# Shifts and scales of the second sub-layer computed with features on partitions

## Chip, cores and metric

The program runs on one core of one Trainium2 chip. The metric is device time in microseconds (us) of one launch, the median of several runs.

## What is computed

One decoder layer on 512 tokens of width 1024. A conditioning vector c gives, for each of the two sub-layers (token mixing and MLP), a shift, a scale and a gate of 1024 numbers each: six rows of a 1024 by 6144 product. Cut to what matters:

```python
c_act = jax.nn.silu(c)
mod = c_act @ w_ada[l] + b_ada[l]
sh1, sc1, g1, sh2, sc2, g2 = jnp.split(mod, 6, axis=-1)
h = rmsnorm(x, norm_gains[l, 0]) * (1.0 + sc1) + sh1
y = token_mixer(h, ...)                    # 8 block-sparse heads, 8 sliding-window heads
x = x + g1 * rmsnorm(y, norm_gains[l, 1])
h = rmsnorm(x, norm_gains[l, 2]) * (1.0 + sc2) + sh2
y = square(relu(h @ w1 + b1)) @ w2 + b2
x = x + g2 * rmsnorm(y, norm_gains[l, 3])
```

The change concerns sh2 and sc2 alone, 2048 dot products of length 1024. The code calls the two sub-layers "layer" 0 and 1.

## The kernel before

Every large product is made of three fp32r matmuls (high by high, high by low, low by high parts, lines 96 to 98), so that each weight tile is split on the way: ACT copies the high part (line 83), POOL or DVE subtracts to get the low part (line 85).

The stages in order of time: the first modulation and the first projections (to about 57 us), then a loop over 64 blocks of attention (lines 802 to 867; 16 heads of 4 blocks of 128 queries; about 63 to 207 us), then the output projection, the residual and the second norm (to about 262 us), then the two MLP products (to about 586 us) and the output.

In the attention loop PE follows the order of the program. In step k it issues the transposes of the block three or four steps back (line 649), the scores of block k (lines 618 and 619), now and then a head's output (line 676), and then matmuls of a "filler" worth 1450 ns (900 ns from k = 24 on): the remaining projections, and later the output projection. The other engines' orders are fixed at build time by a planner that simulates the schedule. A block's chain is: PE scores; DVE adds the bias and takes the minimum (line 626); ACT takes exponentials (line 633); DVE reciprocal (line 639); POOL normalises (line 640); PE transposes. For sliding-window heads POOL first copies a column into the tile (line 617).

Beside this chain run the "side" steps, one call of next(side) each (lines 763 to 776). `ada_wide` computes 1024 sums over the 1024 features of c with c's features on partitions: for each of 8 chunks of c, two DVE instructions of 128x512 (lines 260 and 262) multiply a raw tile by one column of silu(c) and add to `adaacc`; each is one call. What is then left is a sum over the 128 partitions. For a gate (`gate_row`) PE does it with a matmul by ones (line 277). For the second sub-layer's shifts and scales (two units of 1024, r = 1 and 2) PE transposes the eight 128x128 pieces of the accumulator (line 225) and DVE reduces them from PSUM (line 226); `ada_cols` then adds the bias, and forms (1 + scale) * gain with four one-column instructions (line 237). The raw tiles rotate through four buffers (tag araw), and the accumulator has one (tag adaacc).

Calls 1 to 16 are the gate; call 17 closes it and does the first half of unit 1; calls 17 to 32 are unit 1, 33 to 48 unit 2 (33 closes unit 1), 49 closes unit 2. How many calls are made by step k is set in `side_at` (line 773). Each call's DVE instructions are placed in DVE's queue behind the bias instruction of the same step (`behind`).

The first sub-layer's shifts and scales are already computed the other way, in `ada_dot` (line 305): features on partitions, one DVE multiply-and-sum of 128x1024 against silu(c) held on every partition (c_bc).

Of the kernel before, what the change touches and what calls it, by code (L numbers as in the profile page):

```python
# [21 lines left out]
F32 = mybir.dt.float32  # L22
F32R = mybir.dt.float32r
AF = mybir.ActivationFunctionType
ALU = mybir.AluOpType

P = 128
DM = 1024
S = 512
NT = S // P  # L30
KC = DM // P
# [12 lines left out]


@with_exitstack
def layer_kernel(ctx, tc, x, c_col, ada_c, ada_r, bada_col, bada_row, gain_col, gain_row, w_in0, w_in1, w_in2,
                 w_out, w1, b1_col, w2, b2_row, rel, sinks, onehot, out):
    nc = tc.nc

    const = ctx.enter_context(tc.tile_pool(name="const", bufs=1))
    dram = ctx.enter_context(tc.tile_pool(name="dram", bufs=1, space=bass.MemoryType.DRAM))
    small = ctx.enter_context(tc.tile_pool(name="small", bufs=4))
    keep = ctx.enter_context(tc.tile_pool(name="keep", bufs=1))
    wts = ctx.enter_context(tc.tile_pool(name="wts", bufs=2))
# [4 lines left out]
    def bank(name):  # L60
        return psum.tile([P, 512], F32, tag="ps", name=name)
# [110 lines left out]
    gain_c = const.tile([P, 2, KC], F32, name="gain_c")  # L172
# [41 lines left out]

    mods = const.tile([P, 2, KC, 3], F32, name="mods")

    def ada_sums(layer, kcs, acc):

        n = 2 * len(kcs)
        sums = small.tile([P, n], F32, tag=f"sums{n}", name=f"sums{layer}_{kcs[0]}")  # L220
        for h in range(0, n, 4):
            m = min(4, n - h)
            ps = bank(f"adaps{layer}_{kcs[0]}_{h}")
            for s in range(m):
                nc.tensor.transpose(ps[:, s * P:(s + 1) * P], acc[:, (h + s) * P:(h + s + 1) * P], ident)
            nc.vector.tensor_reduce(out=sums[:, h:h + m], in_=ps[:, :m * P].rearrange("p (s q) -> p s q", q=P),
                                    op=ALU.add, axis=mybir.AxisListType.X)
        return sums

    def ada_cols(layer, kcs, ps):  # L230

        n = len(kcs)
        m = mods[:, layer, kcs[0]:kcs[0] + n, :]
        nc.vector.tensor_add(m[:, :, 0:2], ps[:, 0:2 * n].rearrange("p (k s) -> p k s", s=2),
                             bada_c[:, layer, kcs[0]:kcs[0] + n, :])
        for j, kc in enumerate(kcs):
            nc.vector.tensor_scalar(m[:, j, 2:3], m[:, j, 1:2], 1.0, gain_c[:, layer, kc:kc + 1], op0=ALU.add,
                                    op1=ALU.mult)

    def mod(layer, kc):  # L240
        return mods[:, layer, kc, 2:3], mods[:, layer, kc, 0:1]
# [1 line left out]
    def ada_wide(r, pool, then):  # L243

        acc = pool.tile([P, 1024], F32, tag="adaacc", name=f"adaacc{r}", bufs=1)
        raws = []

        def load():
            j = len(raws)
            if j < KC:  # L250
                raws.append(pool.tile([P, 1024], F32, tag="araw", name=f"adar{r}_{j}", bufs=4))
                nc.sync.dma_start(out=raws[j], in_=ada_r[r][:, j * 1024:(j + 1) * 1024])

        for _ in range(3):
            load()
        for j in range(KC):
            load()
            for a, w in zip(halves(acc), halves(raws[j])):
                if j == 0:
                    nc.vector.tensor_scalar_mul(a, w, c_act[:, j:j + 1])  # L260
                else:
                    nc.vector.scalar_tensor_tensor(a, w, c_act[:, j:j + 1], a, op0=ALU.mult, op1=ALU.add)  # L262
                yield
        then(acc)

    def gate_row(layer, g_bc, pool, tag):

# [16 lines left out]
    for h in range(2):  # L284
        ps = bank(f"cbc{h}")
# [57 lines left out]
    for q, ps in enumerate(vec_ps):  # L343
        nc.scalar.activation(vec_sb[:, q, :], ps[0:8, :NVEC], AF.Copy)
    nc.sync.dma_start(out=vec_1.rearrange("q h n -> h q n"), in_=vec_sb)
    nc.gpsimd.tensor_scalar(sink_t, sink_t, -1.0, 1.0, op0=ALU.mult, op1=ALU.mult)

    hh = keep.tile([P, KC, S], F32R, tag="hh", name="hh")
# [413 lines left out]

    def side_steps():
        yield from ada_wide(0, wts, gate_row(0, g_bc, apool, "gt"))
        for r in range(2):
            kcs = list(range(4 * r, 4 * r + 4))
            yield from ada_wide(1 + r, wts, lambda acc: ada_cols(1, kcs, ada_sums(1, kcs, acc)))

    side = side_steps()
    sided = [1]  # L770

    def side_at(k):
        while sided[0] < 4 + min(k, 24) + max(0, min(k, 62) - 24) * 0.7 + max(0, k - 62):
            sided[0] += 1
            with behind() if k < len(blocks) else ExitStack():
                next(side, None)
# [231 lines left out]
    b2_bc = mlp.tile([P, DM], F32, name="b2_bc")  # L1008
    nc.sync.dma_start(out=b2_bc, in_=b2_row.to_broadcast([P, DM]))
    g2_bc = mlp.tile([P, DM], F32, name="g2_bc")  # L1010
    gate = ada_wide(3, wts, gate_row(1, g2_bc, res, "hf"))
    for f in range(3, NF):
        if f < 5:
            ws.make("both")
# [77 lines left out]
def _lay_out(i):  # L1092
# [4 lines left out]
    o["c_col"] = c(a["c"][0].reshape(KC, P).T)  # L1097

    w = a["w_ada"][0].reshape(KC, P, 2, 3, DM)
    cols = lambda l, kcs: np.concatenate(  # L1100
        [w[:, :, l, s, kc * P:(kc + 1) * P] for kc in kcs for s in range(2)], axis=-1)
    unit = lambda m: m.transpose(1, 0, 2).reshape(P, -1)
    wt = a["w_ada"][0].reshape(DM, 2, 3, KC, P)[:, 0, 0:2]
    o["ada_c"] = c(wt.transpose(3, 2, 1, 0).reshape(P, KC * 2 * DM))
    o["ada_r"] = c(np.stack([unit(m) for m in (w[:, :, 0, 2], cols(1, range(4)), cols(1, range(4, 8)), w[:, :, 1, 2])]))
    b = a["b_ada"][0].reshape(2, 3, DM)
    o["bada_col"] = c(b[:, 0:2].reshape(2, 2, KC, P).transpose(3, 0, 2, 1))
    o["bada_row"] = c(b[:, 2])
# [36 lines left out]
```

## Time and profile before

| | us |
|---|---|
| median of 3 runs | 607.13 (605.13 to 607.27) |
| the profiled execution | 606.9 |
| its span, first to last instruction | 605.1 |
| PE, DVE, ACT, POOL busy | 575.3, 322.2, 273.8, 326.7 |

Times in rows are from the start of the span. Matmuls are pipelined: a 128x512 one is shown as 0.39 us long, but the next starts 0.23 us after it, so PE's load is read from starts and from waits rather than from its busy time. A row of waits says engine, tile and line, then who ended the wait, then us in total, times, the longest. A row of stretches gives for each engine the busy time and the count of instructions, then the granted clock of PE (1.00 is 2.4 GHz, 0.5 is 1.2 GHz). A row of time order gives start, duration, engine, line, operation and tiles.

### The profile page before, as it was taken

To read this page: it belongs to the slowest core of one execution; us is meant where nothing else is said; L and a number is where in the kernel's file an instruction comes from. 1 tells how busy PE (TensorE), PEld (TensorE's weight loads), DVE (VectorE), ACT (ScalarE), POOL (GpSimd) and SP (SyncE) were. 2 spreads that over 40 slices of the span, in tenths; PEclk is the share of its full clock that TensorE was granted. 3 is DMA by queue.
4 is the path that set the end of the run, shared out by engine and by line. 5 is a ranking of instruction groups with operands and counts; after the bars stand their busy time and mean duration, and the time that the engine had idled before them with its cause. 6 is when DMAs were issued, how large, how long until landed. Compare 5 with 4: busy or idle time off the path is not lost.

```text
span 605.1 us, 8116 instructions
## 1 busy us (share of the span) xinstructions
PE 575.3 (95%) x2822; PEld 478.7 (79%) x2822; DVE 322.2 (53%) x604; ACT 273.8 (45%) x524; POOL 326.7 (54%) x331
## 2 busy tenths in 40 slices
PE   6899899998879999999999999999999999999994
PEld 3678898877767888988888888788888888888883
DVE  3999899999996746362355555421411111111047
ACT  4646865787775637753322333233423322333122
POOL 2663246577986726365555555755554445546443
PEclk9999999999997999999999999999999999999998
DMA  8994996765664046543334333232223332334105
GB/s 299 407 408 130 220 248 144 138 223 154 191 190 152 1 174 238 180 140 105 104 113 171 135 105 105 69 105 104 86 88 105 105 100 79 102 104 140 36 19 190
DMA packets 29678, 89.31 MB, mean 148 GB/s; under 512 B 3428, under 2 KB 7588, under 8 KB 29637
## 3 DMA queue, kind: packets, MB, share of 16 engines
q1 hardware_dynamic: 28840, 86.55, 44.9%
q10 hardware_dynamic: 668, 2.20, 0.9%
q8 instruction: 22, 0.36, 0.2%
q0 software_dynamic: 128, 0.05, 0.1%
q14 instruction: 20, 0.16, 0.1%
HBM read 84.56 MB, written 4.22 MB: 147 GB/s over the span
## 4 chain that ended last, share of the span: by engine, by line
PE 56%; DVE 2%; ACT 1%; DMA 1%; POOL 1%; issue 1%; DVEq 0%; POOLq 0%; ACTq 0%; SPq 0%
PE u L97 10%; PE u L98 10%; PE u L96 9%; PE y L98 9%; PE y L97 9%; PE y L96 9%; DVE zg L1067 1%; DMA x<-in_x 1%; DVE x L910 0%; POOL wlo L85 0%; DMA out_x<-zg 0%; ACT sq L204 0%; PE adarow L277 0%; ACT h2h L361 0%; POOL zg L1064 0%
## 5 line engine op out<-in xcount | busy, mean ns | idle before, releaser
L85 POOL TENSOR_TENSOR wlo<-raw,whi 128x512 fp32r<-128x512 f32 (+1 forms) x140 | 192.4, 1393 | 157.8 <-ACT whi L83 157.3
L83 ACT ACTIVATE whi<-raw 128x1024 fp32r<-128x1024 f32 (+5 forms) x87 | 80.7, 935 | 130.9 <-PE u L97 109.0
L97 PE MATMUL u<-h2l,whi 128*128 128x512 f32 (+1 forms) x280 | 104.2, 372 | 0.8 <-POOL h2l L363 0.7
L96 PE MATMUL u<-h2h,whi 128*128 128x512 f32 (+1 forms) x280 | 104.7, 374 | 0.0
L98 PE MATMUL u<-h2h,wlo 128*128 128x512 f32 (+1 forms) x280 | 103.8, 371 | 0.0
L97 PE MATMUL y<-wlo,ring_h2h 128*128 128x512 f32 x232 | 90.3, 389 | 0.0
L98 PE MATMUL y<-whi,ring_h2l 128*128 128x512 f32 x232 | 90.3, 389 | 0.0
L96 PE MATMUL y<-whi,ring_h2h 128*128 128x512 f32 x232 | 90.1, 389 | 0.0
L262 DVE SCALAR_TENSOR_TENSOR adaacc<-adar,c_act,adaacc 128x512 f32<-128x512 f32 x56 | 65.9, 1177 | 0.1
L97 PEld LDWEIGHTS u<-h2l,whi 128*128 128x128 f32 x280 | 52.7, 188 | 10.7 <-POOL h2l L363 1.1
L98 PEld LDWEIGHTS u<-h2h,wlo 128*128 128x128 f32 x280 | 52.7, 188 | 9.1
L96 PEld LDWEIGHTS u<-h2h,whi 128*128 128x128 f32 x280 | 52.7, 188 | 9.2 <-ACT whi L83 0.2
L640 POOL TENSOR_SCALAR w<-w,st 128x128 f32<-128x128 f32 (+2 forms) x64 | 38.2, 599 | 38.4 <-DVE st L639 33.1
L97 PEld LDWEIGHTS y<-wlo,ring_h2h 128*128 128x128 f32 x232 | 43.6, 188 | 9.1
L96 PEld LDWEIGHTS y<-whi,ring_h2h 128*128 128x128 f32 x232 | 43.6, 188 | 9.1
L98 PEld LDWEIGHTS y<-whi,ring_h2l 128*128 128x128 f32 x232 | 43.6, 188 | 8.9
L633 ACT ACTIVATE w<-w,st 128x128 f32<-128x128 f32 (+3 forms) x64 | 33.4, 522 | 27.2 <-DVE st L626 25.0
L649 PE MATMUL p<-ident,w 128*128 128x128 f32 x136 | 26.1, 281 | 6.9 <-POOL w L640 6.4
L85 POOL TENSOR_TENSOR w0lo<-w0raw,w0hi 128x384 fp32r<-128x384 f32 x16 | 22.5, 1426 | 12.9 <-ACT w0hi L83 12.9
L649 PEld LDWEIGHTS p<-ident,w 128*128 128x128 f32 x136 | 17.4, 143 | 13.6 <-POOL w L640 9.8
L663 ACT ACTIVATE pth<-p 128x384 fp32r<-128x384 f32 (+3 forms) x48 | 22.2, 466 | 10.4 <-PE p L649 9.9
L305 DVE SCALAR_TENSOR_TENSOR dot<-ada,c_bc 128x1024 f32<-128x1024 f32 (+1 forms) x18 | 24.5, 1362 | 3.3 <-ACT c_bc L289 3.2
(222 smaller groups left out, 1089.6 us busy)
## 6 DMA issues: line engine op xcount, KB each, us to landing
raw<-in_w SPq DMA_DIRECT2D x63, 512.0 KB, 3.3
adar<-in_ada_r SPq DMA_DIRECT2D x32, 512.0 KB, 4.4
ada<-in_ada_c SPq DMA_DIRECT2D x16, 512.0 KB, 9.5
woraw<-in_w_out SPq DMA_DIRECT2D x8, 512.0 KB, 4.4
raw<-in_w_in SPq DMA_DIRECT2D x7, 512.0 KB, 6.7
w0raw<-in_w_in SPq DMA_DIRECT2D x8, 384.0 KB, 9.3
strip<-vec SPq DMA_DIRECT2D x24, 128.0 KB, 4.0
xn<-in_x SPq DMA_DIRECT2D x4, 512.0 KB, 7.9
```

Of the source, the lines that this page charges most:

```text
L83: nc.scalar.activation(hi[:, a:b], src[:, a:b], AF.Copy)
L85: return eng.tensor_sub(lo[:, a:b], src[:, a:b], f32(hi[:, a:b])).ins
L96: nc.tensor.matmul(ps, lh, rh, start=start, stop=False, **kw)
L97: nc.tensor.matmul(ps, lh, rl, start=False, stop=False, **kw)
L98: nc.tensor.matmul(ps, ll, rh, start=False, stop=stop, **kw)
L262: nc.vector.scalar_tensor_tensor(a, w, c_act[:, j:j + 1], a, op0=ALU.mult, op1=ALU.add)
L305: nc.vector.scalar_tensor_tensor(junk[:, cs], ada_raws[kc][b][:, cs], 1.0, c_bc[:, cs], op0=ALU.mult, op1=ALU.mult, accum_out=acc)
L633: anchor["act"] = nc.scalar.activation(w[:, :m], w[:, :m], AF.Exp, bias=st[:, 0:1], scale=-1.0, accum_out=st[:, 1:2]).ins
L640: nc.gpsimd.tensor_scalar(w[:, :n], w[:, :n], st[:, 2:3], 1.0, op0=ALU.mult, op1=ALU.mult)
L649: nc.tensor.transpose(p_ps[:, (c0 + j) * P:(c0 + j + 1) * P], self.w[i][:, j * P:(j + 1) * P], ident)
L663: nc.scalar.activation(dst(self.pth), src, AF.Copy)
L1067: nc.vector.scalar_tensor_tensor(zg[:, cs], zg[:, cs], r3, x1[i][:, cs], op0=ALU.mult, op1=ALU.add)
```

## The change

The two units of sums over c become sixteen dot products per partition. The weights of sh2 and sc2 are laid out (outside the kernel's time) with output features on partitions, as those of the first sub-layer are. silu(c), which lies on every partition in c_bc early in the kernel, is written as one row of 4 KB to DRAM, and read back to all partitions into the accumulator's buffer once the gate has left it. Each of calls 17 to 32 is then one 128x1024 multiply-and-sum, in place in the raw tile; call 33 adds the bias and forms all eight scales with one instruction. The pace of the calls is 0.7 a step from k = 0 to 62, where it was 1 a step to k = 24 and 0.7 behind that. The first sub-layer's one-column instruction becomes the same new form, with one column.

```diff
-    def ada_sums(layer, kcs, acc):
-        ...
-            for s in range(m):
-                nc.tensor.transpose(ps[:, s * P:(s + 1) * P], acc[:, (h + s) * P:(h + s + 1) * P], ident)
-            nc.vector.tensor_reduce(out=sums[:, h:h + m], in_=ps[:, :m * P].rearrange("p (s q) -> p s q", q=P),
-                                    op=ALU.add, axis=mybir.AxisListType.X)
...
-        for j, kc in enumerate(kcs):
-            nc.vector.tensor_scalar(m[:, j, 2:3], m[:, j, 1:2], 1.0, gain_c[:, layer, kc:kc + 1], op0=ALU.add,
-                                    op1=ALU.mult)
+        nc.vector.scalar_tensor_tensor(m[:, :, 2], m[:, :, 1], 1.0, gain_c[:, layer, kcs[0]:kcs[0] + n], op0=ALU.add,
+                                       op1=ALU.mult)
...
+    c_row = dram.tile([1, DM], F32, name="c_row")
+
+    def ada_columns(pool):
+
+        c2 = pool.tile([P, DM], F32, tag="adaacc", name="c_bc2", bufs=1)
+        nc.sync.dma_start(out=c2, in_=c_row.to_broadcast([P, DM]))
+        sums = small.tile([P, KC, 2], F32, name="sums1", bufs=1)
+        raws = []
+
+        def load():
+            j = len(raws)
+            if j < 2 * KC:
+                raws.append(pool.tile([P, 1024], F32, tag="araw", name=f"adak_{j}", bufs=4))
+                nc.sync.dma_start(out=raws[j], in_=ada_k[:, j * 1024:(j + 1) * 1024])
+
+        for _ in range(3):
+            load()
+        for j in range(2 * KC):
+            load()
+            nc.vector.scalar_tensor_tensor(raws[j], raws[j], 1.0, c2, op0=ALU.mult, op1=ALU.mult,
+                                           accum_out=sums[:, j // 2, j % 2:j % 2 + 1])
+            yield
+        ada_cols(1, list(range(KC)), sums.rearrange("p k s -> p (k s)"))
...
+    nc.sync.dma_start(out=c_row, in_=c_bc[0:1, :])
...
         yield from ada_wide(0, wts, gate_row(0, g_bc, apool, "gt"))
-        for r in range(2):
-            kcs = list(range(4 * r, 4 * r + 4))
-            yield from ada_wide(1 + r, wts, lambda acc: ada_cols(1, kcs, ada_sums(1, kcs, acc)))
+        yield from ada_columns(wts)
...
-        while sided[0] < 4 + min(k, 24) + max(0, min(k, 62) - 24) * 0.7 + max(0, k - 62):
+        while sided[0] < 4 + min(k, 62) * 0.7 + max(0, k - 62):
```

## Rows read from the trace of the kernel before

**Rows 1.** The page's 40 slices of the span, VectorE's busy tenths.
```profile
DVE  3999899999996746362355555421411111111047
```

**Rows 2.** Stretches of the loop: PE, PEld, DVE, ACT, POOL; clock; DMA share, GB/s.
```profile
63.00:113.00 50.00, 47.25 (x293) 42.77 (x292) 47.58 (x122) 33.34 (x89) 23.64 (x29) 1.00 0.84 184
113.00:158.00 45.00, 40.99 (x227) 33.42 (x226) 43.47 (x111) 34.99 (x87) 33.74 (x45) 1.00 0.63 182
158.00:189.50 31.50, 26.50 (x140) 21.71 (x139) 27.26 (x72) 21.05 (x51) 28.69 (x43) 0.89 0.67 199
189.50:207.00 17.50, 17.50 (x110) 15.15 (x109) 14.04 (x47) 11.99 (x31) 10.43 (x24) 1.00 0.10 33
```

**Rows 3.** PE's waits from 113 to 158 us.
```profile
PE p L649 <- POOL w L640: 3.7, 5, 1.6
```

**Rows 4.** PE's waits from 158 to 189.5 us.
```profile
PE p L649 <- POOL w L640: 3.3, 4, 1.2
PE y L97 <- POOL wo_hl L85: 1.6, 2, 1.3
PE y L97 <- DVE wloo L85: 0.7, 1, 0.7
```

**Rows 5.** The same columns for the first MLP product.
```profile
262.00:421.00 159.00, 159.00 (x701) 130.96 (x700) 71.99 (x54) 49.49 (x62) 90.80 (x62) 1.00 0.34 113
```

**Rows 6.** Blocks 18, 37 and 39: scores' last matmul, then the bias instruction.
```profile
110.47 0.34 PE L619 MATMUL s<-kkl,q 128*128 128x384 f32 x1
112.34 0.56 DVE L626 CUSTOM_DVE_ANT_0 w<-s,strip 128x384 f32<-128x384 f32 x1
...
152.58 0.28 PE L619 MATMUL s<-kbl,q 128*128 128x256 f32 x1
156.98 0.46 DVE L626 CUSTOM_DVE_ANT_0 w<-s,strip,sink_t 128x256 f32<-128x256 f32 x1
...
158.09 0.28 PE L619 MATMUL s<-kbl,q 128*128 128x256 f32 x1
159.50 0.46 DVE L626 CUSTOM_DVE_ANT_0 w<-s,strip,sink_t 128x256 f32<-128x256 f32 x1
```

**Rows 7.** Line 262 from 113 to 158: shortest, median, longest in ns; then as group.
```profile
L262 DVE SCALAR_TENSOR_TENSOR adaacc<-adar,c_act,adaacc x14: 739/1062/1832, 112.8 to 155.6; 128x512 f32<-128x512 f32 x14
L262 DVE SCALAR_TENSOR_TENSOR adaacc<-adar,c_act,adaacc 128x512 f32<-128x512 f32 x14 | 15.6, 1111 | 0.0
```

**Rows 8.** VectorE in order of time: two dots of the first sub-layer.
```profile
41.41 1.88 DVE L305 SCALAR_TENSOR_TENSOR dot<-ada,c_bc 128x1024 f32<-128x1024 f32 x1
...
43.82 1.21 DVE L305 SCALAR_TENSOR_TENSOR dot<-ada,c_bc 128x1024 f32<-128x1024 f32 x1
...
45.07 0.85 DVE L234 TENSOR_TENSOR mods<-sums,bada_c 128x2 f32<-128x2 f32 x1
```

**Rows 9.** VectorE in order of time: a reduction of unit 1 and its successor.
```profile
139.35 0.68 DVE L226 TENSOR_REDUCE sums<-adaps 128x4 f32<-128x512 f32 x1
139.95 0.55 DVE L664 TENSOR_TENSOR ptl<-p,pth 128x384 fp32r<-128x384 f32 x1
```

**Rows 10.** POOL's one-column copy, 158 to 189.5 us, then 195 to 225 us.
```profile
L617 POOL COPY w<-sink_t 128x1 f32<-128x1 f32 x14 | 7.4, 536 | 1.7 <-PE p L649 1.7
...
L617 POOL COPY w<-sink_t 128x1 f32<-128x1 f32 x6 | 1.1, 182 | 2.5 <-PE p L649 2.5
```

**Rows 11.** PE in order of time, 187.8 to 190.7 us.
```profile
187.82 0.63 PE L97 MATMUL y<-wo_hl,oth 128*128 128x512 f32 x1
188.25 0.63 PE L98 MATMUL y<-wo_hh,otl 128*128 128x512 f32 x1
...
189.85 1.04 PE L225 MATMUL adaps<-ident,adaacc 128*128 128x128 f32 x8
190.64 0.48 PE L96 MATMUL y<-whio,oth 128*128 128x512 f32 x1
```

**Rows 12.** Issue to landing of the transfer of one DRAM row to 128 partitions (line 268).
```profile
DMA to landing us min/median/max: 6.0/6.0/6.0
```

More of the change, by code (lines that the diff above doesn't have):

```diff
@@ L46, in layer_kernel @@
 @with_exitstack
-def layer_kernel(ctx, tc, x, c_col, ada_c, ada_r, bada_col, bada_row, gain_col, gain_row, w_in0, w_in1, w_in2,
+def layer_kernel(ctx, tc, x, c_col, ada_c, ada_k, ada_r, bada_col, bada_row, gain_col, gain_row, w_in0, w_in1, w_in2,
                  w_out, w1, b1_col, w2, b2_row, rel, sinks, onehot, out):
@@ L215, in layer_kernel @@
     mods = const.tile([P, 2, KC, 3], F32, name="mods")
-    def ada_sums(layer, kcs, acc):
[L219 to L223, printed above, removed]
-            for s in range(m):
-                nc.tensor.transpose(ps[:, s * P:(s + 1) * P], acc[:, (h + s) * P:(h + s + 1) * P], ident)
-            nc.vector.tensor_reduce(out=sums[:, h:h + m], in_=ps[:, :m * P].rearrange("p (s q) -> p s q", q=P),
-                                    op=ALU.add, axis=mybir.AxisListType.X)
-        return sums
     def ada_cols(layer, kcs, ps):
@@ L1010, in layer_kernel @@
     g2_bc = mlp.tile([P, DM], F32, name="g2_bc")
-    gate = ada_wide(3, wts, gate_row(1, g2_bc, res, "hf"))
+    gate = ada_wide(1, wts, gate_row(1, g2_bc, res, "hf"))
     for f in range(3, NF):
@@ L1099, in _lay_out @@
     w = a["w_ada"][0].reshape(KC, P, 2, 3, DM)
-    cols = lambda l, kcs: np.concatenate(
-        [w[:, :, l, s, kc * P:(kc + 1) * P] for kc in kcs for s in range(2)], axis=-1)
     unit = lambda m: m.transpose(1, 0, 2).reshape(P, -1)
-    wt = a["w_ada"][0].reshape(DM, 2, 3, KC, P)[:, 0, 0:2]
-    o["ada_c"] = c(wt.transpose(3, 2, 1, 0).reshape(P, KC * 2 * DM))
-    o["ada_r"] = c(np.stack([unit(m) for m in (w[:, :, 0, 2], cols(1, range(4)), cols(1, range(4, 8)), w[:, :, 1, 2])]))
+    for k, l in (("ada_c", 0), ("ada_k", 1)):
+        m = a["w_ada"][0].reshape(DM, 2, 3, KC, P)[:, l, 0:2]
+        o[k] = c(m.transpose(3, 2, 1, 0).reshape(P, KC * 2 * DM))
+    o["ada_r"] = c(np.stack([unit(w[:, :, l, 2]) for l in range(2)]))
     b = a["b_ada"][0].reshape(2, 3, DM)
```

## The prediction, made before the changed kernel was run

> **What bounds the kernel now.** I read the stages first. From 262 us on PE never stops: 701 matmuls in 159 us, one every 0.227 us [rows 5], so what is gained or lost ahead of 190 us is handed on to the end unchanged. The slices show VectorE at 9 tenths from some 15 to 195 us [rows 1], which is the attention loop and what precedes it. I cut the loop by its score matmuls into stage I (blocks 0 to 18, 63 to 113 us), II (19 to 38, to 158 us), III (39 to 52, to 189.5 us) and the rest.
>
> PE's waits and DVE's load are then set side by side. In I DVE is busy 47.6 of 50 us and PE hardly waits. In II DVE is busy 43.5 of 45 us [rows 2], and PE waits 3.7 us for normalised blocks [rows 3]. POOL ends these waits, but it is idle for a quarter of II, and the lateness is born on DVE: the bias instruction starts 1.5 us after block 18's scores are done (110.47 + 0.34 to 112.34), 4.1 us after block 37's, 1.1 us after block 39's [rows 6]. Some 3 to 4 us of this lag is where PE stops. In III PE waits 3.3 us for blocks and 2.3 us for split output weights [rows 4], and the granted clock averages 0.89 [rows 2], that is about 6.9 us at the 1.2 GHz level ((1 - 0.89) x 2 x 31.5). There a 128x512 matmul takes 0.43 us from start to start (187.82 to 188.25 [rows 11]) against 0.23. The clock fell behind the stretch with III's waits. From 189.5 us to the loop's end PE doesn't wait.
>
> So DVE's queue, and in III POOL's beside it, hold PE back in II and III. What a cut of DVE work is worth depends on which stage it is cut from.
>
> **How the calls move.** By line 773, calls made by the end of I (k = 18): before 22, after 17. By the end of II (k = 38): before 38, after 31. Call 32, the last dot, falls at k = 39, call 33 at k = 41; before, calls 39 to 48 were made in III and beyond. So stage I loses 5 calls, II has 14 dots where it had 16 halves and the closing of unit 1, and III has one dot where it had ten halves.
>
> **What one call costs.** A half takes 0.74 us undisturbed, 1.83 at worst, 1.11 on average in II [rows 7], so it waits 0.37. A dot undisturbed is the second of a pair in the first sub-layer: 1.21 us, with the read of its sum 1.25 us from start to start (43.82 to 45.07); the first of the pair takes 1.88, since POOL is splitting a tile at that time [rows 8]. An instruction's successor starts some 0.08 us before its shown end (139.35 + 0.68, then 139.95 [rows 9]), so two undisturbed halves fill 1.32 us; the form alone gains almost nothing; the gain is that a wait is met once per 1024 elements and not twice. I take 1.25 + 0.37 = 1.62 us for a dot in II and III, bounds 1.25 and 1.91 (1.25 + 0.66, the longer of the pair). The nearest row for the wait is line 262's own, since it has the same neighbours on POOL.
>
> The rows show the wait on both sides: POOL's one-column copy takes 0.54 us in III and 0.18 us when no side step runs [rows 10]. The Trainium skill (SBUF — State Buffer, Who interferes with whom) calls this an exclusive lock: a DVE instruction with two SBUF inputs and a GpSimd one that reads SBUF don't run together, and whoever comes second waits out the whole first instruction. By it a dot waits as often as a half does, which gives the 1.62; were the port shared by bandwidth, the wait would double with the elements and a dot would cost 1.25 + 0.74 = 1.99, 5 us more over II. The same rule speaks against the change for POOL, which would be shut out for 1.2 us at a time and not 0.74.
>
> **Stage I.** DVE loses 6 halves of between 0.74 and 1.11 us [rows 7], I take 0.9, and gains one dot, 5.4 - 1.6 = 3.8 us less. PE isn't waiting on DVE here, so that is worth nothing by itself, but block 18's lag of 1.5 us should be gone at the door of II. The new transfer of c to all partitions starts when the gate's sums have left the buffer, takes some 6.0 us by its likeness [rows 12], and stands at the door of I and II; if DVE's order puts the first dot too early, DVE stands for up to 6 us with the next block's bias queued behind it, and the chain to PE with that. The relief in I covers most; I take +0.5, bounds 0 and +4. The 4 KB write, and the sixteen raw loads in place of sixteen, cost SP's queue two more issues; nothing waits for them, 0. A load now frees its buffer after one instruction instead of two, 0.
>
> **Stage II.** Before: 14 halves at 1.11, two first halves (one multiply each, counted as 0.8), two reductions of 0.68 [rows 9], five small ones, 0.7 together; less 23 overlaps of 0.08, 17.3 us. After: 14 x 1.62 = 22.7. DVE gets 5.4 us more work in a stage in which it has none to spare. 1.4 us is covered by the lag that no longer comes in. About 2 us can be left lying at its end, since the lag there is 1.1 us now and PE stops at 3 to 4. The rest, +2.0 us, PE waits; bounds 0 (14 x 1.25 = 17.5, no more than now) and +6 (14 x 1.91 = 26.7, that is 9.4 less 1.4 and 2). The eight transposes in II stand in a queue that DVE holds back, so they are worth 0.
>
> **Stage III.** DVE loses ten halves (about 9.4 us) and gains one dot: its 27.3 us [rows 2] fall to some 19.5, with 2 us brought in, so it is no longer the bound. PE's four waits for blocks go: 3.3 us, and as a shown matmul runs 0.16 us into the next (0.39 against 0.23) some 0.6 more, 3.9. Of the waits for output weights (2.3 and 0.5 hidden), which also hang on ACT's copies, I take half, 1.4. The low clock costs up to 6.9 x (1 - 0.23/0.43) = 3.2 us; I take half, 1.6, because no row shows how few waits would keep it up. Sum -6.9, bounds -9.9 and -2.8 (the time by which POOL's 28.7 us busy fall short of 31.5). POOL is next: of its 28.7 us the copies alone lose 14 x (0.536 - 0.182) = 5.0 to DVE, so it comes to some 23 us, just inside the 24.6 that III would take.
>
> **Behind III.** The eight transposes at 189.85 us take 0.79 us of PE [rows 11] with nothing hiding them: -0.8. Their two reductions and the four small ones lie on DVE where it has time: 0.
>
> **Sum.** +0.5 + 2.0 - 6.9 - 0.8 = -5.2 us against the profiled execution of 606.9 (span 605.1 and 1.8 around it), 601.7. The median of the runs lies 0.2 above it: 601.9.
>
> **Rivals.** (a) POOL takes over in III. For it: it is busy 28.7 of 31.5 us, and DVE's weight splits shut it out too. Against it: the copies' 5.0 us of lost time goes with the halves. Then III gains no more than 31.5 - 28.7 = 2.8, and the sum is +0.5 + 2.0 - 2.8 - 0.8 = -1.1, against the median 606.0, no change that shows. (b) Slower: stage II is overfilled. If a dot meets a running POOL instruction nearly each time (1.91 us), PE's waits there grow by 6 us to about 10 in 45; from some 8 on, the density of III's waits, I expect the clock to fall to 1.2 GHz there, 3.2 us more. III then keeps -4, as it starts with the full lag: +0.5 + 6 + 3.2 - 4 - 0.8 = +4.9, 612.0. Against it: the worst wait each time is not what line 262 shows. (c) The work in II costs PE nothing and all of III's waits and the clock come back: -9.9 - 0.8 = -10.7, 596.4. (d) The planner orders DVE otherwise, so that dots don't stand where the calls put them; then the split by stages fails, and only the total holds: 32 halves and four reductions (some 35 us) against 16 dots (26), 9 us less on DVE. I count its chance in the others.
>
> **How the numbers follow.** Forecast 0.50 (599 to 604), (a) 0.26, (b) 0.16, (c) 0.08. The range goes from 597.0 to 610.0: below it lies half of (c), above it most of (b). About 0.5%, 3 us, is what a measurement of this kernel tells from no change. Faster than that 0.58, within it 0.26, slower 0.16.
>
> **What would show it.** Right: no DVE side work behind about 165 us; PE's waits in III under 2 us and the clock at 1.00 there; in II waits for blocks of 4 to 7 us; dots of 1.2 to 1.9 us, mean near 1.55; everything behind 190 us shifted alike. Wrong: a dot that stands for c's row; PE's waits in II above 8 us or a fallen clock there (b); POOL without idle time in III while DVE has some (a).

## The result, and the profile after

The changed kernel takes 611.04 us (median of 4 runs, 610.17 to 613.05), the kernel before 606.24 us beside it (605.13 to 607.27): a ratio of 1.010, with a 95% interval of 1.0075 to 1.0125. It is slower, and the time lies above the range. The profiled execution took 611.37 us with a span of 609.6, 4.5 us more than the span of before.

In the kernel after, a line of the attention loop stands eleven further down than before: the bias instruction is L637, the normalisation L651, the transposes L660, the one-column copy L628. The new dots are L271. I cut the loop at the same score matmuls as before. The stretches, with the columns of [rows 2]:

```profile
65.00:113.90 48.90, 47.64 (x297) 43.48 (x297) 43.17 (x118) 34.97 (x92) 22.46 (x30) 1.00 0.82 177
113.90:166.60 52.70, 41.73 (x217) 33.55 (x215) 46.20 (x120) 33.64 (x83) 40.85 (x45) 0.97 0.75 222
166.60:194.10 27.50, 25.16 (x141) 20.83 (x139) 18.94 (x58) 20.66 (x49) 22.25 (x41) 0.94 0.43 140
194.10:210.80 16.70, 16.16 (x99) 13.81 (x97) 12.31 (x40) 11.84 (x30) 11.54 (x25) 1.00 0.10 32
```

The cuts in [rows 2] are rounded to the half microsecond. Read to a tenth from the starts of the score matmuls in both traces, the span divides as follows; the start contains the arrival of x and lies between 16.1 and 18.8 us in the traces here (16.4, 17.6 and 17.8 in three kernels whose code is the same up to there).

| stretch, us | before | after | difference |
|---|---|---|---|
| start to the first matmul of the first projections | 17.8 | 16.2 | -1.6 |
| first projections (first sub-layer's modulation beside them) | 38.0 | 42.1 | +4.1 |
| to block 0 | 7.3 | 7.3 | 0 |
| I, blocks 0 to 18 | 50.3 | 48.4 | -1.9 |
| II, blocks 19 to 38 | 44.5 | 52.6 | +8.1 |
| III, blocks 39 to 52 | 31.6 | 27.5 | -4.1 |
| blocks 53 to 63 | 17.0 | 16.7 | -0.3 |
| to the end | 398.6 | 398.9 | +0.3 |

Two places lose, the first projections and stage II. PE's waits of the kernel after, in II and then in III (columns as in [rows 3] and [rows 4]):

```profile
PE p L660 <- POOL w L651: 11.0, 8, 2.1
...
PE p L660 <- POOL w L651: 3.4, 2, 2.1
PE y L97 <- POOL wo_hl L85: 0.6, 2, 0.3
PE y L97 <- DVE wloo L85: 0.4, 1, 0.4
```

In II PE's waits for normalised blocks grow from 3.7 us [rows 3] to 11.0. But DVE is busy 46.20 of 52.70 us there, so it now stands idle for 6.5 us where it was 1.5 before [rows 2], while POOL is busy for 40.85 us where it was 33.7 [rows 2], with 45 instructions both times. They aren't quite the same 45: two products of the gate (2.5 us) have come in, one weight split and one normalisation have left. Of the nine shapes that both have, six take longer and three shorter. A pair of kernels with the same 45 instructions follows among the experiments. POOL's normalisations in II, grouped by shape (busy us, mean ns, then idle time before them), first of before and then of after:

```profile
L640 POOL TENSOR_SCALAR w<-w,st 128x256 f32<-128x256 f32 x6 | 2.9, 478 | 2.1 <-DVE st L639 1.9
L640 POOL TENSOR_SCALAR w<-w,st 128x384 f32<-128x384 f32 x4 | 2.4, 588 | 1.2 <-DVE st L639 1.0
```

```profile
L651 POOL TENSOR_SCALAR w<-w,st 128x256 f32<-128x256 f32 x6 | 5.4, 897 | 0.6 <-DVE st L650 0.6
L651 POOL TENSOR_SCALAR w<-w,st 128x384 f32<-128x384 f32 x3 | 3.7, 1248 | 0.3 <-DVE st L650 0.3
```

The two shapes take 0.90 and 1.25 us where they took 0.48 and 0.59. In order of time one sees which instruction does it:

```profile
136.42 1.94 POOL L651 TENSOR_SCALAR w<-w,st 128x256 f32<-128x256 f32 x1
...
136.80 1.21 DVE L271 SCALAR_TENSOR_TENSOR adak<-adak,c_bc 128x1024 f32<-128x1024 f32 x1
```

A normalisation of 0.48 us overlaps a dot of 1.21 us and lasts 1.94. Which of the two goes first isn't plain from the rows: the normalisation is shown to start 0.38 us ahead of the dot, and yet the dot takes no longer than undisturbed. The dots themselves, in II as a group and then from the source line (shortest, median, longest):

```profile
L271 DVE SCALAR_TENSOR_TENSOR adak<-adak,c_bc 128x1024 f32<-128x1024 f32 x16 | 22.0, 1379 | 0.8 <-DMA c_bc<-c_row 0.8
L271 DVE SCALAR_TENSOR_TENSOR adak<-adak,c_bc x16: 1210/1221/2300, 116.3 to 164.3; 128x1024 f32<-128x1024 f32 x16
```

All sixteen lie in II, where the prediction had counted fourteen, at a mean of 1.38 us, below the 1.62 of the sum. It is POOL that pays, and the normalisation is a link in each block's chain.

The first projections show the other loss. The first sub-layer's one-column instruction for the seven chunks behind the first, before, and in its new form after (source line, ns):

```profile
L237 DVE TENSOR_SCALAR mods<-mods,gain_c x7: 214/214/216, 22.6 to 50.6; 128x1 f32<-128x1 f32 x7
```

```profile
L223 DVE SCALAR_TENSOR_TENSOR mods<-mods,gain_c x7: 931/941/944, 21.0 to 52.4; 128x1 f32<-128x1 f32 x7
```

In the order of time of the kernel after, the one for the first chunk, then one of the seven with its neighbours, then the second sub-layer's:

```profile
10.74 0.16 DVE L223 SCALAR_TENSOR_TENSOR mods<-mods,gain_c 128x1 f32<-128x1 f32 x1
...
41.86 1.01 POOL L85 TENSOR_TENSOR w0lo<-w0raw,w0hi 128x384 fp32r<-128x384 f32 x1
41.95 0.94 DVE L223 SCALAR_TENSOR_TENSOR mods<-mods,gain_c 128x1 f32<-128x1 f32 x1
42.81 1.21 DVE L315 SCALAR_TENSOR_TENSOR dot<-ada,c_bc 128x1024 f32<-128x1024 f32 x1
42.98 0.78 ACT L388 ACTIVATE hh<-tp,mods 128x512 fp32r<-128x512 f32 x1 [3.06 <-DVE mods L223]
...
43.81 0.96 PE L421 MATMUL qk<-hh,w0hi 128*128 128x512 f32 x3 [0.40 <-ACT hh L388]
...
170.14 0.15 DVE L223 SCALAR_TENSOR_TENSOR mods<-mods,gain_c 128x8 f32<-128x8 f32 x1
```

One number per partition takes 0.94 us, while POOL is splitting a tile for all that time; ACT waits for the number, and PE for ACT. The same instruction for the first chunk, at 10.74 us with no POOL instruction beside it, takes 0.16, and on eight columns, in the second sub-layer at 170 us, 0.15. The kernel before met the same split, but with the dot behind: 1.88 us [rows 8], where all the dots behind these seven now take their undisturbed 1.21. So DVE has hardly more to do than before; what is new is that the wait falls ahead of a number that ACT stands for. Seven times 0.73 us is 5.1, of which 4.1 reach PE.

### The profile page after: what moved, and what is told of

It is laid out like the page before. It is cut to its first block, busy times and chain, and to the rows that moved or that the text cites. A ratio compares the mean times of both kernels' runs of the same rounds, so it can differ in the third digit from the quotient of the medians.

```text
span 609.6 us, 8075 instructions
## 1 busy us (share of the span) xinstructions
PE 574.6 (94%) x2806; PEld 477.0 (78%) x2806; DVE 312.1 (51%) x592; ACT 274.0 (45%) x524; POOL 327.6 (54%) x331
## 4 chain that ended last, share of the span: by engine, by line
PE 56%; DVE 2%; ACT 1%; POOL 1%; DMA 1%; issue 1%; DVEq 0%; POOLq 0%; ACTq 0%; SPq 0%
PE u L97 10%; PE u L98 9%; PE u L96 9%; PE y L96 9%; PE y L98 9%; PE y L97 9%; DVE zg L1076 1%; DMA x<-in_x 1%; DVE x L919 0%; POOL wlo L85 0%; DMA out_x<-zg 0%; ACT sq L204 0%; PE adarow L287 0%; POOL zg L1073 0%; ACT hf L373 0%
## 5 line engine op out<-in xcount | busy, mean ns | idle before, releaser
L97 PEld LDWEIGHTS u<-h2l,whi 128*128 128x128 f32 x280 | 52.7, 188 | 10.9 <-POOL h2l L374 1.2
L651 POOL TENSOR_SCALAR w<-w,st 128x128 f32<-128x128 f32 (+2 forms) x64 | 40.4, 636 | 36.6 <-DVE st L650 31.0
L96 PEld LDWEIGHTS u<-h2h,whi 128*128 128x128 f32 x280 | 52.7, 188 | 9.2 <-ACT whi L83 0.2
L98 PEld LDWEIGHTS u<-h2h,wlo 128*128 128x128 f32 x280 | 52.7, 188 | 9.1
L98 PEld LDWEIGHTS y<-whi,ring_h2l 128*128 128x128 f32 x232 | 43.5, 188 | 9.1
L97 PEld LDWEIGHTS y<-wlo,ring_h2h 128*128 128x128 f32 x232 | 43.5, 188 | 9.1
L96 PEld LDWEIGHTS y<-whi,ring_h2h 128*128 128x128 f32 x232 | 43.5, 188 | 8.9
L660 PE MATMUL p<-ident,w 128*128 128x128 f32 x136 | 26.0, 280 | 12.2 <-POOL w L651 12.2
L248 DVE SCALAR_TENSOR_TENSOR adaacc<-adar,c_act,adaacc 128x512 f32<-128x512 f32 x28 | 36.8, 1314 | 0.1
L660 PEld LDWEIGHTS p<-ident,w 128*128 128x128 f32 x136 | 17.5, 143 | 19.5 <-POOL w L651 15.7
L675 DVE TENSOR_TENSOR ptl<-p,pth 128x384 fp32r<-128x384 f32 (+3 forms) x48 | 25.2, 525 | 2.3 <-ACT pth L674 2.1
```

The lines of the kernel that those rows point to most:

```text
L96: nc.tensor.matmul(ps, lh, rh, start=start, stop=False, **kw)
L97: nc.tensor.matmul(ps, lh, rl, start=False, stop=False, **kw)
L98: nc.tensor.matmul(ps, ll, rh, start=False, stop=stop, **kw)
L651: nc.gpsimd.tensor_scalar(w[:, :n], w[:, :n], st[:, 2:3], 1.0, op0=ALU.mult, op1=ALU.mult)
L660: nc.tensor.transpose(p_ps[:, (c0 + j) * P:(c0 + j + 1) * P], self.w[i][:, j * P:(j + 1) * P], ident)
L675: nc.vector.tensor_sub(dst(self.ptl), src, f32(dst(self.pth)))
```

## The experiments

The theory after the two traces: the small form costs the first projections some 4 us, and in II the dots lengthen POOL's part of the chain, because a DVE instruction with two inputs in SBUF and a POOL instruction that reads SBUF shut each other out. Its rivals for II: DVE's queue is simply too full there, as the prediction had it; the calls come at the wrong pace; the transfer of c at the entry of II ("the door") throws the queue back; and the planner, which simulates each kernel anew, puts the queues in another order. Each ratio stands to the kernel before in the same set of runs, with its 95% interval.

### The small form, each way

The changed kernel with the old form in the first sub-layer:

```diff
+        if n == 1:
+            nc.vector.tensor_scalar(m[:, 0, 2:3], m[:, 0, 1:2], 1.0, gain_c[:, layer, kcs[0]:kcs[0] + 1], op0=ALU.add,
+                                    op1=ALU.mult)
+            return
```

> The changed kernel, but the first sub-layer forms its scale (1 + scale) * gain with the old one-column instruction again (one tile input, the gain as a per-partition scalar) and not with the new one (two tile inputs). Theory A: in the first stage the new form waits for POOL's weight split, 0.94 us in place of 0.21 us, seven times, on the path to the next chunk's matmuls: then this kernel is 3 to 4 us faster than the changed kernel's 611.0, 607 to 608, and the first score matmul of attention starts near 62 us in place of 65.6. Rival: the whole 5 us come from the density of the dots in the attention loop; then this kernel stays at 610 to 611.

Measured: 608.65 us (607.68 to 612.15), 1.0082 [1.005, 1.0115]. The first projections are back at 38.0 us, II stays at 52.6. In the experiments that build on this kernel the lines of the loop stand four further down (normalisation L655, transposes L664, dots L275).

The kernel before with the new form alone:

```diff
-        for j, kc in enumerate(kcs):
-            nc.vector.tensor_scalar(m[:, j, 2:3], m[:, j, 1:2], 1.0, gain_c[:, layer, kc:kc + 1], op0=ALU.add,
-                                    op1=ALU.mult)
+        nc.vector.scalar_tensor_tensor(m[:, :, 2], m[:, :, 1], 1.0, gain_c[:, layer, kcs[0]:kcs[0] + n], op0=ALU.add,
+                                       op1=ALU.mult)
```

> The kernel before with the new form of (1 + scale) * gain alone (one two-input instruction for all columns of a call; sums, transposes and pace as before). Theory A: slower than before by 2 to 4 us, 608.5 to 610, all of it ahead of the first score matmul. Rival (density alone): 606, no change.

Measured: 606.93 us, 1.004 [1.0023, 1.0058]; the first projections take 41.6 us in place of 38.0. So this form alone accounts for 0.2 to 0.6%, less than expected, and it isn't the whole loss: with the form undone in the changed kernel, 0.5 to 1.15% is left. Of the 3.6 us lost early, the total keeps some 2.5; in its profiled run stages I and III are 1.4 and 2.2 us shorter than in the profiled run of before, II 0.3 longer. A stage I of 48.9 us thus comes about with all the halves of before in it.

### Too much in II: another pace, and another length

The changed kernel with its dots spread from block 14 to the end:

```diff
-        while sided[0] < 4 + min(k, 62) * 0.7 + max(0, k - 62):
+        while sided[0] < 4 + min(k, 14) + max(0, k - 14) * 0.4:
```

> The changed kernel with another pace: one call a step to k = 14 (the gate), then 0.4 a step, so that the sixteen dots spread over some 40 steps as the 32 halves did, in place of 0.7 a step over 23. Theory B (density: at 0.7 dots a step DVE's and POOL's queues are late in stage II and PE waits): stage II (blocks 19 to 39) falls from 52.7 us to 45 to 48, the total to 604 to 607. Rival C (the form: a dot of 1.2 us blocks POOL's normalising and DVE's own reciprocals each time, whatever the pace): each dot still costs, the cost moves from II to III, and the total stays at 609 to 611.

Measured: 609.28 us (606.05 to 611.01), 1.0075 [1.0052, 1.0098]. II falls to 42.7 us, below the 44.5 of before, and the clock never falls in the loop; but stage I grows to 53.2. VectorE in order of time at the end of I:

```profile
103.17 0.69 DVE L675 TENSOR_TENSOR ptl<-p,pth 128x512 fp32r<-128x512 f32 x1
105.96 1.23 DVE L271 SCALAR_TENSOR_TENSOR adak<-adak,c_bc 128x1024 f32<-128x1024 f32 x1 [2.11 <-DMA c_bc<-c_row]
107.11 0.08 DVE L271 DVE_READ_ACCUMULATOR adak<-adak,c_bc 128x1 f32 x1
107.11 1.22 DVE L271 SCALAR_TENSOR_TENSOR adak<-adak,c_bc 128x1024 f32<-128x1024 f32 x1
108.26 0.08 DVE L271 DVE_READ_ACCUMULATOR adak<-adak,c_bc 128x1 f32 x1
108.26 1.22 DVE L271 SCALAR_TENSOR_TENSOR adak<-adak,c_bc 128x1024 f32<-128x1024 f32 x1
```

Between the end of the work at 103.86 and the dot at 105.96 DVE's queue stands 2.11 us for c's row, and then three dots run one behind the other: 5.6 us without a bias instruction. With eight dots in II in place of sixteen, II is short, as the density would have it. But the door has moved to I, which is 4.8 us longer than in the changed kernel, and the gain in the total (1.010 to 1.0075, with overlapping intervals) is less than expected.

Each dot as two halves of 512 in the same call:

```diff
+        halfs = small.tile([P, 2, KC, 2], F32, name="halfs1", bufs=1)
...
-            nc.vector.scalar_tensor_tensor(raws[j], raws[j], 1.0, c2, op0=ALU.mult, op1=ALU.mult,
-                                           accum_out=sums[:, j // 2, j % 2:j % 2 + 1])
+            for h in range(2):
+                cs = slice(h * 512, h * 512 + 512)
+                nc.vector.scalar_tensor_tensor(raws[j][:, cs], raws[j][:, cs], 1.0, c2[:, cs], op0=ALU.mult,
+                                               op1=ALU.mult, accum_out=halfs[:, h, j // 2, j % 2:j % 2 + 1])
...
+        nc.vector.tensor_add(sums, halfs[:, 0], halfs[:, 1])
```

> The changed kernel at its own pace, each dot made as two halves of 128x512 right behind one another in the same call, and one addition at the end. Rival C (the length of a single instruction is what hurts, as POOL is shut out for 1.2 us at a time): POOL gets in between the halves, stage II becomes 2 to 5 us shorter, total 606 to 609. Theory B (load per step): no gain, 611 to 613, as two halves meet POOL twice and take 0.1 us more.

Measured: 611.84 us, 1.011 [1.0082, 1.0139], the same as the changed kernel. In its profile II is 2.7 us shorter (49.9), some 1.5 of which is the clock (1.00 in place of 0.97), and III is 2.3 longer (29.8). Stage II, with the columns of [rows 2]:

```profile
114.40:164.40 50.00, 40.49 (x217) 32.20 (x215) 47.82 (x140) 33.04 (x81) 37.37 (x44) 1.00 0.72 216
```

DVE is busier here than in the changed kernel (47.82 us against 46.20) and POOL less (37.37 against 40.85), and yet II is shorter, which speaks against DVE's full queue as the cause. Cutting the dots in two doesn't undo the loss; whether the length of a single instruction counts for part of it, this run leaves open.

### The shut-out and the door, one at a time

Three kernels on the base of the one with the old small form. They leave out the true dot products, so the second sub-layer's shifts and scales are other numbers in them; their time is what they are for. The first has sixteen columns of c's row copied in place of the dots, and keeps their loads and calls:

```diff
+        nc.vector.tensor_copy(sums.rearrange("p k s -> p (k s)"), c2[:, 0:2 * KC])
...
-            nc.vector.scalar_tensor_tensor(raws[j], raws[j], 1.0, c2, op0=ALU.mult, op1=ALU.mult,
-                                           accum_out=sums[:, j // 2, j % 2:j % 2 + 1])
```

> The kernel with the old scale, with the sixteen dots left out (the sums are sixteen columns of c's row copied in their place, so that the second sub-layer's shifts and scales are other numbers); transfers, calls and pace stay. It gives what the dots cost in all. If DVE's side work is what holds stages II and III back, stage II falls from 52.6 to 41 to 44 us and the total to 596 to 599. If the pace or the transfers cost, it stays above 603.

Measured: 604.81 us, 1.0009 [0.9994, 1.0023]. It doesn't tell what the dots cost: with nothing to use up the raw tiles in turn, SyncE's queue issues all sixteen loads ahead of the transfer of c's row, and DVE's queue stands 12.7 us for it.

```profile
120.10 0.33 SPq L270 DMA_DIRECT2D adak<-in_ada_k  x1
120.53 1.08 SPq L261 DMA_DIRECT2D c_bc<-c_row  x1
```

That is SyncE's queue in order of time. PE's waits from 110 to 160 us have this line alone, and the clock is at 1.2 GHz for 10.2 us behind it:

```profile
PE proj L96 <- DVE st L640: 8.5, 1, 8.5
```

The second puts in place of each dot an instruction with one SBUF input of the same shape, which also writes a sum; its factor is one number per partition that is there early, so that the wait for c's row goes too. The third takes the factor from c's row, so that the wait is back.

```diff
-            nc.vector.scalar_tensor_tensor(raws[j], raws[j], 1.0, c2, op0=ALU.mult, op1=ALU.mult,
-                                           accum_out=sums[:, j // 2, j % 2:j % 2 + 1])
+            nc.vector.tensor_scalar(raws[j], raws[j], c_act[:, 0:1], 0.0, op0=ALU.mult, op1=ALU.add,
+                                    accum_out=sums[:, j // 2, j % 2:j % 2 + 1])
```

```diff
-            nc.vector.tensor_scalar(raws[j], raws[j], c_act[:, 0:1], 0.0, op0=ALU.mult, op1=ALU.add,
+            nc.vector.tensor_scalar(raws[j], raws[j], c2[:, 0:1], 0.0, op0=ALU.mult, op1=ALU.add,
```

> The kernel with the old scale, each dot replaced by a one-input instruction of the same width that also writes a sum (the raw tile times one column of silu(c); the sums are other numbers). It takes DVE about as long (1.1 to 1.2 us with the read of the sum), but reads one tile. Theory C (DVE and POOL shut each other out): POOL's normalising goes back to 0.4 to 0.6 us, the instruction is never over 1.3 us long, stage II falls from 52.6 to 44 to 48 us, total 602 to 605. Theory B (DVE's own time and its order): stage II stays at 50 or more, total 606 to 608.

> The run with one-input instructions in place of the dots (old scale, sums are other numbers), but each now reads its factor from c's row in the accumulator's buffer, so that it waits for that transfer as the dots do. It parts the two things that run took away at once. Theory C (DVE and POOL shut each other out): nearly all of the gain stays, ratio to before 0.985 to 0.995, stage II 42 to 45 us. Theory D (the wait for c's row at the door of stage II and the dots that pile up behind it): most of the gain goes, ratio 1.00 to 1.005, stage II 47 us or more.

Measured: 598.04 us, 0.9887 [0.9862, 0.9912], without the wait; 601.69 us, 0.9925 [0.9898, 0.9952], with it; against 1.0082 [1.005, 1.0115] for the dots. Of stage II, for each kernel the stretch, the normalisation of two shapes, the instructions in question and PE's wait. Dots (the kernel with the old small form):

```profile
110.40:163.00 52.60, 41.52 (x217) 33.51 (x215) 46.30 (x120) 33.66 (x83) 40.88 (x45) 0.97 0.75 223
...
L655 POOL TENSOR_SCALAR w<-w,st 128x256 f32<-128x256 f32 x6 | 5.4, 897 | 0.6 <-DVE st L654 0.6
...
L655 POOL TENSOR_SCALAR w<-w,st 128x384 f32<-128x384 f32 x3 | 3.8, 1251 | 0.3 <-PE s L634 0.3
...
L275 DVE SCALAR_TENSOR_TENSOR adak<-adak,c_bc x16: 1210/1222/2296, 112.8 to 160.8; 128x1024 f32<-128x1024 f32 x16
...
PE p L664 <- POOL w L655: 11.1, 8, 2.1
```

One input, with the wait for c's row:

```profile
112.00:157.60 45.60, 40.95 (x215) 33.53 (x214) 42.87 (x115) 33.77 (x83) 29.75 (x45) 0.96 0.80 246
...
L655 POOL TENSOR_SCALAR w<-w,st 128x256 f32<-128x256 f32 x6 | 2.9, 483 | 2.0 <-DVE st L654 2.0
...
L655 POOL TENSOR_SCALAR w<-w,st 128x384 f32<-128x384 f32 x3 | 1.8, 588 | 0.3 <-DVE st L654 0.3
...
L275 DVE TENSOR_SCALAR_CACHE_REDUCE adak<-adak,c_bc x16: 1265/1274/1279, 114.5 to 157.9; 128x1024 f32<-128x1024 f32 x16
...
PE p L664 <- POOL w L655: 4.6, 5, 1.9
```

One input, without the wait:

```profile
110.50:152.60 42.10, 39.08 (x215) 32.40 (x214) 40.56 (x112) 33.61 (x83) 29.98 (x46) 1.00 0.84 249
...
L655 POOL TENSOR_SCALAR w<-w,st 128x256 f32<-128x256 f32 x6 | 2.9, 486 | 0.2 <-DVE st L654 0.2
...
L655 POOL TENSOR_SCALAR w<-w,st 128x384 f32<-128x384 f32 x4 | 2.4, 590 | 0.2 <-DVE st L654 0.2
...
L275 DVE TENSOR_SCALAR_CACHE_REDUCE adak<-adak,c_act x16: 1265/1274/1276, 103.5 to 153.5; 128x1024 f32<-128x1024 f32 x16
...
PE p L664 <- POOL w L655: 3.0, 4, 1.0
```

The sixteen instructions still cost DVE 16 x 1.27 = 20.4 us where the dots cost 22.0, so DVE's queue is nearly as full: 1.7 us less, where II gains 7.0. What goes is POOL's: with the wait for c's row kept, 40.9 us busy become 29.8 for the same 45 instructions, shape by shape, the normalisation is at 0.48 and 0.59 us again, PE waits 4.6 in place of the 11.1 us of the dots, and II ends 7.0 us sooner. That is the shut-out; in the total it is 1.6% between the two ratios, whose intervals lie far apart. The planner's orders differ between these two kernels as well: some neighbours in DVE's and ACT's queues change places, and from block 31 on some in POOL's. But 2.0 of the 7.0 us are there by block 22, ahead of the first such difference: PE waits 1.95 us in block 21 with the dots, and not at all there with one input. How much of the rest the orders account for, no run settles. PE's wait in time order, with the dots:

```profile
118.30 0.55 PE L664 MATMUL p<-ident,w 128*128 128x128 f32 x3 [1.95 <-POOL w L655]
```

The wait for c's row adds 0.4% more by the medians; those two intervals overlap a little (0.9898 to 0.9912), so its size is less sure. Without it the planner also places the first instructions earlier, so that thirteen lie in II in place of fifteen. The profiles give 3.5 us of II to both, of which some 1.7 are a fallen clock (0.96 against 1.00: 3.6 us at the lower level, of which 1 - 0.23/0.43 is lost). Another buffer for c's row would take the wait away in the changed kernel itself; that was not tried.

### Where the dots would do less harm

The dots first and the gate behind them, at the pace of the change, and then at an even pace of 0.55 calls a step; and the gate first at that same even pace (all with the old small form):

```diff
-        yield from ada_wide(0, wts, gate_row(0, g_bc, apool, "gt"))
         yield from ada_columns(wts)
+        yield from ada_wide(0, wts, gate_row(0, g_bc, apool, "gt"))
...
-        while sided[0] < 4 + min(k, 62) * 0.7 + max(0, k - 62):
+        while sided[0] < 2 + k * 0.55:
```

> The changed kernel with the old one-column scale in the first sub-layer (as in the run that undid it) and with the sixteen dots ahead of the gate: c's row is then in the buffer before attention begins, and no dot waits for it; pace as in the changed kernel. Theory D (the door): the transfer of c's row cannot start before the gate has left the buffer, so that two or three dots queue up behind it on DVE and run back to back, and that costs 3 to 4 us at the 19th block; it goes: 604.5 to 606 where the kernel with the old scale alone ran 608.65 (before: 604.4). Theory B (density, 0.7 dots a step against 0.7 halves): the dots now lie in blocks 0 to 20, where PE waits little, and the gate's halves in blocks 18 to 42 at the load of before: 603 to 606 too, but with PE's waits moved into blocks 4 to 20, 3 to 5 us of them.

> As the run with the dots ahead of the gate, but at 0.55 calls a step from the first block to the last, so that the side work has one load throughout. Theory B (density): another 1 to 3 us faster than the dots first at 0.7, 601 to 604, which would beat the kernel before by up to 3 us. Theory D alone: no difference to the run with the dots first at 0.7.

> The changed kernel with the old scale in the first sub-layer and 0.55 calls a step, gate first as in the changed kernel. Against the run with the dots first at the same pace (ratio to before 0.990) it shows what the order costs, against the run with the old scale alone (1.008) what the pace gives. Theory B with C (a two-input instruction costs by how often it falls among POOL's per step): ratio 0.990 to 0.997. Theory D (door): 3 to 4 us above the dots first, ratio 0.996 to 1.003.

| | ratio | I | II | III | blocks 53 to 63 | dots from, to |
|---|---|---|---|---|---|---|
| dots first, pace of the change | 1.0093 [1.0066, 1.012] | 59.0 | 43.7 | 28.8 | 16.7 | 55.3, 114.4 |
| dots first, even pace | 0.9904 [0.9884, 0.9925] | 47.7 | 42.8 | 26.4 | 20.0 | 55.1, 121.8 |
| gate first, even pace | 1.0008 [0.9997, 1.002] | 45.7 | 46.4 | 32.6 | 16.9 | 130.8, 187.8 |

At the pace of the change the first dots outrun their loads, and DVE's queue stands 3.83 us for a raw tile, behind block 0's bias instruction:

```profile
68.63 1.23 DVE L275 SCALAR_TENSOR_TENSOR adak<-adak,c_bc 128x1024 f32<-128x1024 f32 x1 [3.83 <-DMA adak<-in_ada_k]
```

Evenly spread and early, the same sixteen dots give 599.38 us (598.13 to 600.52), which beats both kernels. Evenly spread and late, from 130.8 us on, they give 606.39, no change: above what the shut-out alone had let me expect, and in the range of the door. But the first dot waits for c's row for only 0.2 us there, so it isn't the door. Against the kernel with the old small form (1.0082), which has the same order, the pace is worth 0.7%; the order is worth 1% more. With the dots first, I and the last blocks are 2.0 and 3.1 us longer, II and III 3.6 and 6.2 us shorter. POOL's normalisation in III, of one shape, with the gate first and then with the dots first:

```profile
L655 POOL TENSOR_SCALAR w<-w,st 128x256 f32<-128x256 f32 x10 | 9.5, 955 | 1.2 <-DVE st L654 1.1
```

```profile
L655 POOL TENSOR_SCALAR w<-w,st 128x256 f32<-128x256 f32 x10 | 5.6, 566 | 1.0 <-DVE st L654 1.0
```

The stretches of the early version (I and II):

```profile
63.00:110.80 47.80, 45.71 (x292) 42.34 (x290) 45.51 (x125) 34.90 (x92) 20.13 (x28) 1.00 0.92 236
110.80:153.60 42.80, 40.15 (x217) 34.01 (x215) 36.45 (x106) 34.01 (x86) 34.24 (x46) 0.96 0.60 168
```

In I POOL has 28 instructions in 47.8 us, and is idle for more than half of it even with the dots there. In II it has 46 in 42.8 us. That this room is why the dots cost less in I is argued from these rows; no run shows it by itself.

How much of this is the form and how much is pace and order? The kernel before, all halves as they were, first at an even pace of 0.8 and then also with the gate last:

```diff
-        while sided[0] < 4 + min(k, 24) + max(0, min(k, 62) - 24) * 0.7 + max(0, k - 62):
+        while sided[0] < 2 + k * 0.8:
```

```diff
-        yield from ada_wide(0, wts, gate_row(0, g_bc, apool, "gt"))
         for r in range(2):
             kcs = list(range(4 * r, 4 * r + 4))
             yield from ada_wide(1 + r, wts, lambda acc: ada_cols(1, kcs, ada_sums(1, kcs, acc)))
+        yield from ada_wide(0, wts, gate_row(0, g_bc, apool, "gt"))
```

> The kernel before with another pace alone: 0.8 calls a step from the first block to the last, so that its 49 calls end where the 33 of the slow runs end. If the pace is all that the run with the dots first at 0.55 won, and the form of the sums is worth nothing, this one comes out at a ratio of 0.99 to 0.995 too. If half as many two-input instructions are worth something by themselves, it stays at 0.997 to 1.003.

> The kernel before (halves of 128x512, transposes and reductions) at 0.8 calls a step as in the run with the even pace, and with the two units of the second sub-layer ahead of the gate. It is the counterpart of the run with the dots first at 0.55 (ratio 0.990): same order, same end, old form of the sums. If the order alone won that, this one comes out at 0.988 to 0.993 too. If the dots as such win by being half as many two-input instructions, in a place where POOL has idle time, it stays at 0.995 to 1.000.

Measured: 604.41 us, 0.9978 [0.9961, 0.9995], and 602.1 us (601.43 to 603.05), 0.9955 [0.9936, 0.9975]. The intervals of these two overlap, so the order alone is not settled for the old form. Pace and order together are worth some 0.45%, and the dots in the same early place, 0.9904, another 0.5%; there the intervals lie apart by a hair (0.9925 and 0.9936). So in this early place, and at an even pace, the form of the change is a gain of that size.

## Why the prediction was wrong

**The first sub-layer's small form.** The sum has no term for it. The change section says that the one-column instruction takes the new form there too, and the prediction read line 237 only in the second sub-layer, where it has time. In the first it lies between the dot and ACT, seven times, and goes from 0.21 to 0.94 us: +4.1 us in the first projections, shown by the two runs that move this form alone (38.0 us without it, 41.6 with it). The row for the price stood in [rows 8]: the two-input addition in front of it, on two columns, takes 0.85 us there.

**Stage II, the term.** I took +2.0 (0 to +6); it was +8.1. The dots came in below my price (1.38 against 1.62), and the side work in II took 21.0 us of DVE's queue by the trace, for sixteen dots, where I had 22.7 for fourteen. So the queue wasn't costed too low, and the step that failed is the reading that the term rests on: that the lateness is born on DVE, and that POOL, idle for a quarter of II, needn't be priced. I wrote that POOL would be shut out for 1.2 us at a time, and then left it out of the sum. In the runs it was the larger part: with the same 45 POOL instructions in II, the dots keep POOL busy for 40.9 us and PE waiting for 11.1, one-input instructions of nearly the same length for 29.8 and 4.6. The prediction had the rule for it: by the Trainium skill (SBUF — State Buffer, Who interferes with whom) a two-input DVE instruction and a GpSimd one that reads SBUF exclude each other. The trace agrees on POOL's side: 0.48 us became 0.90. The same section of the Trainium skill says that a DVE instruction with at most one SBUF input does not contend, outside the modes that use both port pairs. The one-input runs agree: 486 and 590 ns, and 483 and 588, for the two shapes. A mean idle share of a quarter was no cover, since the normalisation stands in each block's chain and PE waits for its end, not for POOL's mean.

Worked out again with what was measured: PE's waits in II +7.3 us, 0.5 more for three more waits (0.16 each, as in the prediction), the clock, 0.97 over 52.7 us, 3.2 us at the lower level or 1.5 us lost, less the 0.8 of the transposes that left: +8.5, against +8.1. (Over the loop the clock changed little: 3.2 us at the lower level in II and 3.3 in III, against 6.9 in III before.)

**The door.** I took +0.5 (0 to +4). The transfer was issued at 112.7 us and landed 3.5 us later, and the first dot stood 0.8 us for it. That is about the term. But the wait also let two dots run one behind the other, and the run that moved the door into I showed it at its worst; the pair of one-input runs gives it, with the places that go with it, some 0.4%.

**Stage III.** I took -6.9 (-9.9 to -2.8); it was -4.1. The DVE side did what was said: no dot behind 165.8 us, DVE busy 18.9 of 27.5. But II handed its lateness on: PE still waits 3.4 us for blocks, and the clock averages 0.94 there, 3.3 us at the lower level where [rows 2] give 6.9. POOL, rival (a), is busy 22.3 of 27.5 and is not the bound. Two sums of the prediction are a little off here, without changing the term: 28.7 - 5.0 is 23.7 us for POOL, and DVE's 19.5 leaves out the 2 us that are brought in.

**Stage I and behind III.** I had 0 and it was -1.9. Its cause stays open: the kernel before with the new small form alone, which has all its halves, comes to 48.9 us too. Behind III -0.3 in place of -0.8; the start's -1.6 is within what the traces differ by there.

**The rivals.** (b) was the nearest, 612.0 against 611.0: waits of some 10 us in II, a fallen clock there, and -4 left in III, all of which the trace shows. Its mechanism was only half of what happened: it put the price on the dot that meets POOL's instruction (1.91 us), whereas the median dot takes 1.22 and POOL's instruction waits. And its total comes out close partly by chance, since the 4.1 us of the first projections aren't in it, its clock was 3.2 us where 1.5 was lost, and stage I gave 1.9 back. (d) came true in a small way: the dots aren't where the calls put them, sixteen in II and not fourteen.

**What stays open.** By the medians the form in the first sub-layer costs 0.2% when taken out of the change (1.010 to 1.0082, with overlapping intervals) and 0.4% when put alone into the kernel before. How much of its 4 us later stages give back, no run settles: the runs of one kernel already spread over 3.7 us for the kernel before (602.45 to 606.18 in one set), with a mean granted clock of 0.995 in the shortest and 0.989 in the longest of them.

## What to carry to other kernels

Price a two-input DVE instruction on both engines: beside its own time, ask which POOL instruction that reads SBUF waits it out, and whether that one stands in a chain that PE waits for. Put such work where POOL has few instructions, at an even pace, and not right behind a transfer into a reused buffer, because DVE's queue stands for it and then runs what has piled up in one piece. When a helper is edited, look up every one of its callers in the trace: here a caller that the change wasn't made for cost as much in the trace as stage III gained.

## What was not expected of the hardware

- A two-input DVE instruction of one column took 0.93 to 0.94 us, seven times of seven, each beside a POOL split, against 0.21 us for the form with one tensor input beside the same split, and 0.16 us for the same form where no POOL instruction ran. In these seven its time is that of the POOL instruction it meets, not of its size.
- The one-input multiply with a running sum took 1.265 to 1.279 us for 128x1024 in all 32 cases of two runs, with some 45 POOL instructions beside it in stage II, while the dot took 1.21 to 2.30. It is 0.05 us dearer than the undisturbed dot, and steady.
- DVE's busy share fell in the stage that got more DVE work (43.5 of 45 us to 46.2 of 52.7). An engine that becomes less busy can still be the cause, by way of another.
